# Eight pairs by seven quarter products in place of six, in the first MLP product of an encoder layer

## The chip, the cores and the metric

The kernel runs on one core of one Trainium2 chip. The metric is the device time of one execution in microseconds (us), given as the median of several runs. The engines are called as in the profile: PE (TensorE, matrix products), PEld (its weight loads), DVE (VectorE), ACT (ScalarE), POOL (GpSimd) and SP (SyncE, which here only issues DMAs).

## What is computed

One layer of a streaming encoder: four token mixers, a cross-attention, and a gated MLP, for 512 tokens of width 1024 in float32. The change lies in the MLP, whose inner width is 2816:

```python
hf = _rms_norm(x, norm_ffn_pre[l])
u = _dwconv_causal(hf @ w_up[l], ffn_dw[l]) + ffn_dw_b[l]
u_g, u_v = jnp.split(u, 2, axis=-1)
yff = (jax.nn.silu(u_g) * u_v) @ w_down[l]
x = x + _rms_norm(yff, norm_ffn_post[l])
```

The first MLP product is `hf @ w_up`. Column block j of 128 columns exists twice, once as gate and once as value; the two are called pair j, and there are 22 pairs (0 to 21).

## The kernel before

**Numbers.** Each float32 operand is split into a high part (an ACT cast to a shorter format, `wh`) and the rest (a DVE subtraction, `wl`). A product is three matmuls per block of 128 rows: high by high, high by low, low by high (`mm3`, line 240).

**A plain pair** takes two weight tiles of 128x1024 (gate, value), and per tile 8 row blocks x 3 matmuls of 512 columns: 48 such matmuls. DVE then adds two shifted taps of the convolution (line 597), ACT gives the first tap with its bias and the silu (lines 1612, 1618), DVE multiplies gate by value (line 1619).

**A pair by seven quarter products** treats gate and value, two halves of the inner width and two halves of the tokens as 2x2 blocks, and replaces eight block products by seven (names A11, A12, S1, S2, S3, S4, A22), at the price of sums. Each product has 4 row blocks x 3 matmuls of 256 columns: 84 such matmuls for the pair. The sums of token parts are made once (`token_terms`). The sums of weights are four DVE additions per pair (lines 1691 to 1694, tiles `su`, `wv`, `s4`), the sums of results are three ACT copies and three DVE additions to `u` (line 1684), with one more copy.

**A turn.** `SEVEN_AT` lists the pairs j that are done in this way, and each such pair shares a turn with the plain pair j+1 (`seven_jobs`, line 1665 on). A turn has five weight tiles, split in this order. I call them by a letter:

- F: A11 and A12 (from `wg`)
- G: the gate tile of pair j+1 (from `wr`)
- S: S1 and S2 (from `su`)
- T: S3 and A22 (from `wv`)
- V: the value tile of pair j+1 (from `wr`)

S4 has tiles of its own (`s4h`, `s4l`). F of turn 8 is written F8, and so on. A turn does 84 matmuls of 256 columns and 48 of 512.

**Slots.** Split weights have four slots (`weights_tile`): the n-th weight tile of the program takes slot n mod 4, so its ACT cast waits until PE has done the last matmul on the tile four before it. With turns back to back, V of a turn follows F of that turn in its slot, F of the next turn follows G, the next G follows S, the next S follows T, and the next T follows V:

```python
        return w_tiles.pop((kind, i), None) or gp.tile([P, WB], F32R, tag=f"{kind}{i % 4}", name=kind)
```

Raw weights from HBM have two buffers (`wr`), loaded by SP; `wg`, `wv`, `su` and the tiles of the next paragraph (`wp`) share a ring of seven buffers.

**Steps.** During the first product, the kernel also prepares the weights of the second one (`Sums`, line 530 on): for each of 11 row pairs q, POOL loads two tiles `wp` from `w_down`, DVE does four operations on them (lines 545 to 548), POOL stores them to `sums`. Each call of `step()` does the next load, the next four operations or the next store: two loads, then 11 times add, store and (9 times) load, 33 in all. A turn calls `step()` four times, a plain pair twice from pair 3 on.

**Order.** The program is written in turn order, and a scheduler then places the instructions of each engine by a model of its own, once, when the kernel is built. On the chip every engine takes its instructions in that fixed order.

Of the kernel before, what the change touches and what calls it, by code (L numbers as in the profile page):

```python
# [36 lines left out]
WB = 2 * 520  # L37
LINE = 256
HALF_SHIFT = 16
SEVEN_AT = (4, 7, 10, 13, 16, 19)  # L40
BIG = -float(2.0 ** 100)
LAMBDA_INIT = 0.8 - 0.6 * math.exp(-0.3 * 0)

# [41 lines left out]
def hybrid_layer(ctx: ExitStack, tc: tile.TileContext, a: dict, out: bass.AP):  # L85
# [12 lines left out]
    def bank(tag=None):  # L98
        if tag is None:
            turn_of.n += 1  # L100
            tag = "av" if turn_of.shared and turn_of.n % 2 else "mm"
        return psum.tile([P, 512], F32, tag=tag, name=f"ps_{tag}", bufs=2)
# [50 lines left out]
    def split(ps, hi, lo, scale=None):  # L153

        if scale is None:
            A.copy(hi, ps)  # L156
            V.tensor_tensor(lo, ps, hi.bitcast(F32), ALU.subtract)  # L157
        else:
            A.activation(hi, ps, AF.Copy if isinstance(scale, float) else AF.Identity, scale=scale)
            V.scalar_tensor_tensor(lo, ps, scale, hi.bitcast(F32), ALU.mult, ALU.subtract)  # L160
# [19 lines left out]
    def split_weights(raw, shape, low=V, order=same, shift=0):  # L180

        n = int(math.prod(shape[1:]))
        hi, lo = weights_tile("wh"), weights_tile("wl")
        names = "k c" if len(shape) == 3 else "c"
        form = f"p ({names}) -> p {names}"

        def view(t):
            return t.rearrange(form, k=shape[1]) if len(shape) == 3 else t

        hi, lo = hi[:, shift:shift + n], lo[:, shift:shift + n]  # L190
        order(A.copy(hi, raw[:, :n]))  # L191
        low.tensor_tensor(lo, raw[:, :n], hi.bitcast(F32), ALU.subtract)  # L192
        return view(hi), view(lo)
# [38 lines left out]
    def matmul(ps, lhs, rhs, start, stop, more=False):  # L232
        PE.matmul(ps, lhs, rhs, start=start, stop=stop, skip_group_check=more)  # L233
        bg.clock += max(int(math.prod(rhs.shape[1:])), 256) * 0.00042
# [1331 lines left out]
    def ring(dtype=F32, name="dw"):  # L1566
        return ns.fp.tile([P, D], dtype, tag="dw", name=name, bufs=7)
# [37 lines left out]
    def up_jobs():  # L1605
        st, held = {}, []
        seven = SEVEN_AT
        raws = {}

        def first_and_taps(c, j, i, src):  # L1610
            ch = i * NF + j
            st["first"] = A.activation(c[:, i], src, AF.Identity, bias=pc("fb", ch), scale=pc("fdw2", ch)).ins
            st["taps"] = taps(c[:, i], src, lambda k: pc("fdw01", k * 44 + ch), 3).ins
# [8 lines left out]
        def done(j, i, ps):  # L1622
            if i == 0:
                st[j] = ns.fp.tile([P, 2, S], F32, tag="c", name="c", bufs=2)
            first_and_taps(st[j], j, i, ps)
            if i == 1:
                gated(st[j], j)
# [14 lines left out]
        def step(n=1):  # L1642
            for _ in range(n):
                f, q = next(steps, (None, None))
                if f == ns.sums.add:
                    with tc.issue_after(st["taps"]):
                        f(q)
                elif f is not None:
                    f(q)

        def half_sums(ps, w, ks):
            hi, lo = w
            for k in ks:
                mm3(ps, hi[:, k], lo[:, k], ns.hf[0][:, k], ns.hf[1][:, k], k == 0, k == NK - 1)
# [4 lines left out]
        def load_pair(j):  # L1659
            if j in seven:  # L1660
                raws[j] = [ring(name="wg"), ring(name="wv")]
                for i, raw in enumerate(raws[j]):
                    SP.dma_start(raw.rearrange("p (k c) -> p k c", k=NK), plain(j, i)[0])

        def seven_jobs(j):
            n, tok = j + 1, [slice(i * S // 2, (i + 1) * S // 2) for i in range(2)]
            w, x, kept = {}, {}, {}
            old = lambda k, t: [h[:, 4 * k:4 * k + 4, tok[t]] for h in ns.hf]

            def weights(name, raw):  # L1670
                hi, lo = split_weights(raw, [P, NK, P], V, same, HALF_SHIFT)
                for i, m in enumerate(name):
                    w[m] = hi[:, 4 * i:4 * i + 4], lo[:, 4 * i:4 * i + 4]
                return ()

            def product(ps, name, b, first=True):
                hi, lo = w[name]
                for k in range(4):
                    for i, (w_p, x_p) in enumerate(((hi, b[0]), (hi, b[1]), (lo, b[0]))):
                        matmul(ps[:, :S // 2], w_p[:, k], x_p[:, k], first and i == k == 0, i == 2 and k == 3,  # L1680
                               not first)

            def add(dst, ps):
                V.tensor_tensor(dst, dst, ps[:, :S // 2], ALU.add)

            def first_weights():
                g, v = raws[j]
                su, s4 = kept["su"], kept["s4"] = ring(name="su"), ns.fp.tile([P, S], F32, tag="s4", name="s4")
                weights(("A11", "A12"), g)
                with tc.issue_after(st["taps"]):  # L1690
                    V.tensor_tensor(su[:, :S], v[:, :S], v[:, S:], ALU.add)
                V.tensor_tensor(su[:, S:], su[:, :S], g[:, :S], ALU.subtract)
                V.tensor_tensor(v[:, :S], g[:, :S], v[:, :S], ALU.subtract)
                V.tensor_tensor(s4, g[:, S:], su[:, S:], ALU.subtract)
                return [()]

            def second_weights():
                load_pair(seven[seven.index(j) + 1] if j < seven[-1] else None)
                weights(("S1", "S2"), kept["su"])
                return [()]  # L1700

            def third_weights():
                weights(("S3", "A22"), raws.pop(j)[1])
                hi, lo = (ns.fp.tile([P, S + 64], F32R, tag=f"s4{m}", name=f"s4{m}") for m in "hl")
                hi, lo = (m[:, HALF_SHIFT:HALF_SHIFT + S] for m in (hi, lo))
                split(kept["s4"], hi, lo)
                w["S4"] = tuple(m.rearrange("p (k c) -> p k c", k=4) for m in (hi, lo))
                return [()]

            def first(_):  # L1710
                u = kept["u"] = ns.fp.tile([P, 2, 2, S // 2], F32, tag="u", name="u", bufs=2)
                x.update(x=bank("sc"), v=bank("sc"), w=bank("tr"))
                product(x["x"], "A11", old(0, 0))
                A.copy(u[:, 0, 0], x["x"][:, :S // 2])
                product(x["w"], "A12", old(1, 0))
                add(u[:, 0, 0], x["w"])

            def gate_first(hi, lo):
                x["n"] = bank(), (hi, lo)
                half_sums(*x["n"], range(4))  # L1720
                step()

            def second(_):
                product(x["x"], "S2", ns.terms[1], False)
                A.copy(kept["u"][:, 1, 0], x["x"][:, :S // 2])
                step()

            def third(_):
                u = kept["u"]
                product(x["v"], "S3", ns.terms[2])  # L1730
                half_sums(*x["n"], range(4, NK))
                done(n, 0, x["n"][0])
                product(x["x"], "S1", ns.terms[0], False)
                A.copy(u[:, 1, 1], x["x"][:, :S // 2])
                add(u[:, 1, 1], x["v"])
                step()

            def value(hi, lo):
                u, ps = kept["u"], bank()
                half_sums(ps, (hi, lo), range(4))  # L1740
                product(x["x"], "S4", old(1, 1), False)
                A.copy(u[:, 0, 1], x["x"][:, :S // 2])
                half_sums(ps, (hi, lo), range(4, NK))
                done(n, 1, ps)
                step()
                product(x["v"], "A22", ns.terms[3], False)
                add(u[:, 1, 0], x["v"])
                c = ns.fp.tile([P, 2, S], F32, tag="c", name="c", bufs=2)
                for i in range(2):
                    first_and_taps(c, j, i, u[:, i].rearrange("p a b -> p (a b)"))  # L1750
                gated(c, j)

            yield first_weights, None, first
            yield *plain(n, 0), gate_first, V, same, 0
            yield second_weights, None, second
            yield third_weights, None, third
            yield *plain(n, 1), value, V, same, 0
# [30 lines left out]
        j = 0  # L1788
# [250 lines left out]
```

## Time and profile before

| | us |
|---|---|
| median of 3 runs | 1046.9 (1046.65 to 1046.99) |
| the profiled execution's own time | 1047.96 |
| its span, first to last instruction | 1046.2 |
| PE busy | 1036.5 (99%) |
| DVE busy | 836.9 (80%) |
| ACT busy | 530.6 (51%) |
| turn 4's first product starts, from the span's start | 743.9 |

The profiled execution lies 1.06 us above the median, and 1.8 us of its time lie outside of the span. All rows quoted in the prediction are of this one execution. A row of the timeline gives start, duration, engine, line, operation, destination and sources, and in brackets how long the engine stood idle before it and what ended that.

### The profile page before, as it was taken

How to read it: one execution, taken by the hardware profiler on the slowest of the kernel's cores; microseconds unless marked ns; L12 is line 12 of the kernel's file. 1: busy time of each engine (PE TensorE's matmuls, PEld its weight loads, DVE VectorE, ACT ScalarE, POOL GpSimd, SP SyncE). 2: the span in 40 equal slices, each digit the busy share in tenths (PEclk: the TensorE clock that was granted, in tenths of full speed). 3: DMA queues.
4: the chain of work that ended last, by engine and by line, in shares of the span. 5: the costliest groups of instructions: out<-in, count | busy, mean ns of one | idle time of the engine just before them, and what ended most of it. 6: DMA issues, size and time to landing. Idle time of an engine off the chain costs nothing.

```text
span 1046.2 us, 15153 instructions
## 1 busy us (share of the span) xinstructions
PE 1036.5 (99%) x5511; PEld 891.6 (85%) x5511; DVE 836.9 (80%) x1386; ACT 530.6 (51%) x894; POOL 181.6 (17%) x309
## 2 busy tenths in 40 slices
PE   9999999999999999999999999999999999999997
PEld 8888888888888988888888899999888888888886
DVE  6899998667667567767577888788898888889996
ACT  5322222277565356655443665676445443566772
POOL 4000000300230334342112033020011111000031
PEclk9999999999999999999999999999999999999999
DMA  7953433652343263322457743246577767757652
GB/s 254 301 177 104 104 101 125 188 131 81 106 134 95 76 177 102 101 83 79 121 153 229 267 136 122 81 138 206 174 229 242 237 218 233 242 176 220 199 175 81
DMA packets 166528, 167.31 MB, mean 160 GB/s; under 512 B 6655, under 2 KB 136300, under 8 KB 166197
## 3 DMA queue, kind: packets, MB, share of 16 engines
q1 hardware_dynamic: 154147, 124.10, 39.8%
q0 software_dynamic: 12160, 42.10, 12.0%
q8 instruction: 43, 0.70, 0.3%
q14 instruction: 32, 0.26, 0.1%
q10 hardware_dynamic: 146, 0.14, 0.0%
HBM read 141.13 MB, written 25.18 MB: 159 GB/s over the span
## 4 chain that ended last, share of the span: by engine, by line
PE 98%; DMA 1%; DVE 0%; issue 0%; ACT 0%; POOLq 0%; DVEq 0%; POOL 0%; SPq 0%; ACTq 0%
PE ps_mm L233 48%; PE ps_av L233 28%; PE ps_sc L233 13%; PE ps_tr L233 5%; PE ps_tr L237 2%; DMA wide<-in_w_out 1%; PE ps_mm L445 1%; PE ps_mm L387 0%; PE ps_sc L392 0%; PE ps_av L445 0%; ACT hth L156 0%; DVE o L1923 0%; PE ps_tr L429 0%; DVE wide L546 0%; POOLq L2035 0%
## 5 line engine op out<-in xcount | busy, mean ns | idle before, releaser
L191 ACT CAST wh<-wr 128x1024 fp32r<-128x1024 f32 (+1 forms) x130 | 136.3, 1050 | 235.8 <-PE ps_mm L233 129.2
L192 DVE TENSOR_TENSOR wl<-wr,wh 128x1024 fp32r<-128x1024 f32 (+1 forms) x130 | 161.1, 1241 | 65.5 <-ACT wh L191 65.3
L233 PE MATMUL ps_mm<-hth,wh 128*128 128x512 f32 (+1 forms) x544 | 202.6, 380 | 0.2 <-ACT hth L156 0.2
L233 PE MATMUL ps_mm<-htl,wh 128*128 128x512 f32 (+1 forms) x544 | 202.4, 379 | 0.0
L233 PE MATMUL ps_mm<-hth,wl 128*128 128x512 f32 (+1 forms) x544 | 202.1, 379 | 0.0
L233 PEld LDWEIGHTS ps_mm<-hth,wl 128*128 128x128 f32 x544 | 100.5, 188 | 18.2
L233 PEld LDWEIGHTS ps_mm<-hth,wh 128*128 128x128 f32 x544 | 100.6, 188 | 17.8 <-ACT hth L156 0.8
L233 PEld LDWEIGHTS ps_mm<-htl,wh 128*128 128x128 f32 x544 | 100.6, 188 | 17.0
L233 PE MATMUL ps_av<-hth,wh 128*128 128x512 f32 (+1 forms) x304 | 113.2, 373 | 0.0
L233 PE MATMUL ps_av<-htl,wh 128*128 128x512 f32 (+1 forms) x304 | 113.2, 372 | 0.0
L233 PE MATMUL ps_av<-hth,wl 128*128 128x512 f32 (+1 forms) x304 | 113.1, 372 | 0.0
L668 DVE SCALAR_TENSOR_TENSOR y<-y,par,y 128x482 f32<-128x482 f32 (+29 forms) x120 | 83.3, 735 | 0.1
L233 PEld LDWEIGHTS ps_av<-hth,wl 128*128 128x128 f32 x304 | 57.1, 188 | 10.0
L233 PEld LDWEIGHTS ps_av<-hth,wh 128*128 128x128 f32 x304 | 57.2, 188 | 9.7
L233 PEld LDWEIGHTS ps_av<-htl,wh 128*128 128x128 f32 x304 | 57.1, 188 | 9.8
L1808 ACT CAST wh<-dw 128x1024 fp32r<-128x1024 f32 x32 | 33.2, 1050 | 18.3 <-PE ps_tr L233 9.0
L269 POOL TENSOR_TENSOR st_m<-pm,nhalf 128x1 f32<-128x1 f32 x12 | 13.5, 1128 | 159.5 <-ACT junk L1878 90.4
L1809 DVE TENSOR_TENSOR wl<-dw,wh 128x1024 fp32r<-128x1024 f32 x32 | 39.0, 1222 | 2.8 <-ACT wh L1808 2.3
L1061 POOL TENSOR_SCALAR fbias<-ck,cq 128x128 f32<-128x128 f32 (+3 forms) x32 | 28.2, 890 | 63.0 <-DVE st L1068 56.6
L156 ACT CAST pth<-ps_tr 128x512 fp32r<-128x512 f32 (+3 forms) x56 | 23.5, 448 | 24.9 <-PE ps_tr L237 24.7
L233 PE MATMUL ps_sc<-t,wh 128*128 128x256 f32 x168 | 32.8, 278 | 0.0
L157 DVE TENSOR_TENSOR ptl<-ps_tr,pth 128x512 fp32r<-128x512 f32 (+3 forms) x56 | 27.5, 512 | 6.0 <-ACT pth L156 5.7
(553 smaller groups left out, 2453.2 us busy)
## 6 DMA issues: line engine op xcount, KB each, us to landing
wr<-in_w_in SPq DMA_DIRECT2D x38, 512.0 KB
wr<-in_w_gate SPq DMA_DIRECT2D x32, 512.0 KB
wr<-in_w_up SPq DMA_DIRECT2D x32, 512.0 KB
wp<-in_w_down POOLq DMA_DIRECT2D x22, 512.0 KB, 4.6
sums<-wp POOLq DMA_DIRECT2D x22, 512.0 KB, 3.7
dw<-sums SPq DMA_DIRECT2D x44, 256.0 KB
wr<-in_w_branch SPq DMA_DIRECT2D x16, 512.0 KB
wide<-in_w_out SPq DMA_DIRECT2D x12, 512.0 KB
```

The lines of the kernel that those rows point to most:

```text
L156: A.copy(hi, ps)
L157: V.tensor_tensor(lo, ps, hi.bitcast(F32), ALU.subtract)
L191: order(A.copy(hi, raw[:, :n]))
L192: low.tensor_tensor(lo, raw[:, :n], hi.bitcast(F32), ALU.subtract)
L233: PE.matmul(ps, lhs, rhs, start=start, stop=stop, skip_group_check=more)
L237: PE.transpose(ps, x, ident[:n, :n])
L269: G.tensor_tensor(m, parts[0], eps[:, :n], ALU.add)
L445: keep(PE.matmul(banks[c][:, :S // 2], w[p == 1][:, k, c * P:(c + 1) * P], ht[p == 2][:, i * 4 + k, :S // 2], start=(i, p, k) == (0, 0, 0) ...
L668: ins = V.scalar_tensor_tensor(dst[:, s:], src[:, :S - s], pc("conv_dw", k * 4 + j), dst[:, s:], ALU.mult, ALU.add)
L1061: G.tensor_scalar(bias[:, :w], ck[j][:, :w], -1.0, cq[:, qt, head:head + 1], ALU.mult, ALU.add)
L1808: A.copy(hi, x)
L1809: parts["low"] = V.tensor_tensor(lo, x, hi.bitcast(F32), ALU.subtract).ins
```

## The change

Turns are at pairs 4, 6, 8, 10, 12, 14, 16 and 19 in place of 4, 7, 10, 13, 16 and 19. So the plain pairs 6, 9, 12 and 15 between turns go, pair 18 remains, and seven turns follow each other directly. In the turns at 4, 6 and 8, `step()` is called a fifth time, in `first`.

```diff
-SEVEN_AT = (4, 7, 10, 13, 16, 19)
+SEVEN_AT = (4, 6, 8, 10, 12, 14, 16, 19)
...
                 A.copy(u[:, 0, 0], x["x"][:, :S // 2])
+                if j < 10:
+                    step()
                 product(x["w"], "A12", old(1, 0))
```

The scheduler places the instructions anew. Two places matter below. Numbers in names tell tiles apart.

**First place: the end of turn 6.** On ACT before, this is how the cast of T7 (`wh_7611`) stood; that of G7 (`wh_7532`) stood ten rows ahead of it:

```order
L191 CAST wh_7573<-su_7453 128x1024 [waits PE_49]
L1618 ACTIVATE c_7521<-c_7521 128x512 [waits DVE_49,Activation_49]
L1612 ACTIVATE c_7561<-ps_mm_7536,par2_411 128x512 [waits DVE_49,PE_49]
L191 CAST wh_7611<-wv_7278 128x1024 [waits DMAHW6_49,PE_49]
L1612 ACTIVATE c_7561<-ps_av_7577,par2_411 128x512 [waits PE_49]
```

Now, on ACT, `wh_7753` is T8, which takes the slot of V of turn 6, `wh_7628` is G8, which takes the slot of S6, and `c_7656` belongs to pair 7:

```order
L191 CAST wh_7601<-wg_7459 128x1024 [waits DMAHW0_49,PE_49]
L1612 ACTIVATE c_7656<-ps_mm_7584,par2_411 128x512 [waits PE_49]
L1727 COPY u_7544<-ps_sc_7545 128x256 [waits PE_49]
L191 CAST wh_7753<-wv_7460 128x1024 [waits DVE_49,DMAHW2_49,PE_49,Activation_49]
L1618 ACTIVATE c_7656<-c_7656 128x512 [waits DVE_49,Activation_49]
L191 CAST wh_7628<-wr_7626 128x1024 [waits DMAHW1_49,PE_49]
```

T8's cast now stands two rows ahead of G8's. On PE before, after the last of the 12 matmuls of A12 (into `ps_tr`), the first matmul with a new gate tile has no wait of its own left:

```order
L233 MATMUL ps_tr_7622<-htl_6456,wh_7455 128x256
L233 MATMUL ps_tr_7622<-hth_6455,wl_7456 128x256
L233 MATMUL ps_mm_7655<-hth_6455,wh_7532 128x512
L233 MATMUL ps_mm_7655<-htl_6456,wh_7532 128x512
L233 MATMUL ps_mm_7655<-hth_6455,wl_7533 128x512
```

Now, on PE, the last matmul of V6 (`ps_av_7686`) is followed by the 12 of A12 of turn 8, and the last of these by the first with G8:

```order
L233 MATMUL ps_tr_7764<-htl_6456,wh_7601 128x256
L233 MATMUL ps_tr_7764<-hth_6455,wl_7602 128x256
L233 MATMUL ps_mm_7801<-hth_6455,wh_7628 128x512 [waits Activation_49]
L233 MATMUL ps_mm_7801<-htl_6456,wh_7628 128x512
L233 MATMUL ps_sc_7545<-hth_6455,s4h_7540 128x256 [waits Activation_49]
```

So the first G8 matmul now waits for ACT itself, and A12 of the next turn runs ahead of S4 of this one.

**Second place: the start of turn 10.** On ACT before, the cast of V of turn 10 (`wh_7943`, in the slot of F10) came right behind the copy of A11's result:

```order
L1618 ACTIVATE c_7853<-c_7853 128x512 [waits DVE_49,Activation_49]
L1714 COPY u_7911<-ps_sc_7912 128x256 [waits PE_49]
L191 CAST wh_7943<-wr_7941 128x1024 [waits DMAHW7_49,PE_49]
L1725 COPY u_7911<-ps_sc_7912 128x256 [waits PE_49]
L191 CAST wh_7964<-wr_7962 128x1024 [waits DMAHW0_49,PE_49]
```

Now, on ACT, `wh_7899` is S10 (in the slot of T8), `wh_8033` is F12 and `wh_8012` is V10:

```order
L191 CAST wh_7899<-su_7818 128x1024 [waits PE_49]
L1612 ACTIVATE c_8088<-ps_mm_8016,par2_411 128x512 [waits DVE_49]
L191 CAST wh_8033<-wg_7895 128x1024 [waits DMAHW1_49]
L1612 ACTIVATE c_7963<-u_7761,par2_411 128x512 [waits DVE_49]
L191 CAST wh_8012<-wr_8010 128x1024 [waits DMAHW7_49,PE_49]
L1714 COPY u_7980<-ps_sc_7981 128x256 [waits PE_49]
```

Four ACT operations that start with S10's cast now stand ahead of V10's. On PE, now, S3 of turn 10 (`ps_sc_7982`) is followed by two matmuls of A12 of turn 12 and then by V10; before, the 24 of V stood behind the last of their gate tile. The rows now:

```order
L233 MATMUL ps_sc_7982<-t0_7146,wl_7973 128x256
L233 MATMUL ps_tr_8196<-hth_6455,wh_8033 128x256 [waits Activation_49]
L233 MATMUL ps_tr_8196<-htl_6456,wh_8033 128x256
L233 MATMUL ps_av_8118<-hth_6455,wh_8012 128x512 [waits Activation_49]
L233 MATMUL ps_av_8118<-htl_6456,wh_8012 128x512
L233 MATMUL ps_sc_7981<-t6_7142,wh_7899 128x256 [waits Activation_49]
```

Both V10's first matmul and F12's first wait for ACT.

## The prediction

> **What bounds the kernel now.** I read the busy times first, then the chain of work that ended last, then the stretches of the first MLP product one by one.
>
> ```profile
> PE 1036.5 (99%) x5511; PEld 891.6 (85%) x5511; DVE 836.9 (80%) x1386; ACT 530.6 (51%) x894; POOL 181.6 (17%) x309
> ...
> PE 98%; DMA 1%; DVE 0%; issue 0%; ACT 0%; POOLq 0%; DVEq 0%; POOL 0%; SPq 0%; ACTq 0%
> ```
>
> PE is busy throughout and is the chain that ends last. The windows of two whole periods (a turn and the plain pair behind it; columns are length, then busy time of PE, PEld, DVE, ACT and POOL, granted clock, DMA share, GB/s) say the same of the place of the change: PE never rests there, DVE rests 31.63 - 27.03 = 4.60 us.
>
> ```profile
> 786.08:817.70 31.62, 31.62 (x181) 27.77 (x181) 27.03 (x38) 14.96 (x21) 4.26 (x8) 1.00 0.73 233
> 817.70:849.33 31.63, 31.63 (x182) 27.78 (x181) 27.03 (x38) 14.95 (x21) 3.19 (x6) 1.00 0.68 217
> ```
>
> So time can be won only by giving PE less to do, and is lost wherever PE comes to wait. The chain gives PE's pace (start, length, what):
>
> ```profile
> 801.88 5.44 PE ps_av L233 x24
> 807.32 1.41 PE ps_sc L233 x12
> 808.73 1.41 PE ps_tr L233 x12
> ...
> 833.51 5.44 PE ps_av L233 x24
> ```
>
> 24 matmuls of 512 columns take 5.44 us, 0.227 each. 12 of 256 take 1.41, 0.118 each. A period is 833.51 - 801.88 = 31.63.
>
> **What PE is spared.** A plain pair is 2 x 5.44 = 10.88. A period holds two plain pairs and one pair by seven, so the latter takes 31.63 - 21.76 = 9.87 (84 x 0.118 agrees: 9.9). Each pair changed over saves 1.01, two save **2.02 us**. This is PE's whole gain; the bytes from HBM and the 33 steps stay the same in number, so nothing else gets shorter on the path.
>
> **What DVE gets.** A turn alone lasts 31.63 - 10.88 = 20.75 on PE. DVE's own pace is read from starts, since one operation's record runs on into the next:
>
> ```profile
> 782.67 0.69 DVE L547 TENSOR_TENSOR wp<-wp 128x512 f32<-128x512 f32 x1
> 783.40 0.69 DVE L548 TENSOR_TENSOR wp<-wp 128x512 f32<-128x512 f32 x1
> ...
> 795.30 1.22 DVE L192 TENSOR_TENSOR wl<-wr,wh 128x1024 fp32r<-128x1024 f32 x1
> 796.44 0.69 DVE L1694 TENSOR_TENSOR s<-wg,su 128x512 f32<-128x512 f32 x1
> 797.04 0.74 DVE L597 SCALAR_TENSOR_TENSOR c<-ps_av,par,c 128x510 f32<-128x510 f32 x1
> 797.70 0.68 DVE L548 TENSOR_TENSOR wp<-wp 128x512 f32<-128x512 f32 x1
> 798.30 0.74 DVE L597 SCALAR_TENSOR_TENSOR c<-u,par,c 128x510 f32<-128x510 f32 x1
> 798.96 0.41 DVE L1684 TENSOR_TENSOR u<-u,ps_sc 128x256 f32<-128x256 f32 x1
> 799.29 0.74 DVE L597 SCALAR_TENSOR_TENSOR c<-ps_av,par,c 128x511 f32<-128x511 f32 x1
> ```
>
> From start to start a weight tile's low part takes 1.14, an operation of 512 columns 0.60, a tap 0.66, an addition to `u` 0.33. A turn has 5 low parts (5.7), 7 operations of 512 (four weight sums, the low part of S4, two gated products: 4.2), 8 taps (5.3) and 3 additions (1.0): 16.2 us. Four steps of the sums of `w_down` per turn are 4/3 of a row pair at 4 x 0.60 = 2.4, so 3.2; five steps are 4.0. DVE is then busy 19.4 us, in turns 4, 6 and 8 20.2 us, of PE's 20.75. Before, it was 27.03 of 31.63. So DVE keeps up on the whole, with 0.5 to 1.3 us of rest per turn. I cost its added work (about 5 us per changed pair) at nothing, because PE's matmuls cover it; without that cover it would cost what exceeds 20.75, which the second rival takes up. POOL's two more DMAs per row pair come at the same rate of steps; SP's five loads per turn of two pairs replace loads of the same bytes.
>
> **What the tighter turns add: waits for a slot.** Slots rule when a split can begin. The clearest case of before is a cast that waits for PE's last matmul on the slot, and the low part that waits for the cast:
>
> ```profile
> 786.56 1.05 ACT L191 CAST wh<-wr 128x1024 fp32r<-128x1024 f32 x1 [2.60 <-PE ps_mm L233]
> ...
> 787.64 1.23 DVE L192 TENSOR_TENSOR wl<-wr,wh 128x1024 fp32r<-128x1024 f32 x1 [3.56 <-ACT wh L191]
> ```
>
> These waits cost nothing before, since PE needed the tile only several us later. With the plain pair gone, a release and the need of the next tile come closer, and then the rows ahead of a cast on ACT count. ACT's pace, again from start to start:
>
> ```profile
> 796.85 0.82 ACT L1612 ACTIVATE c<-u,par 128x512 f32<-128x512 f32 x1
> 797.57 0.61 ACT L156 CAST s4h<-s 128x512 fp32r<-128x512 f32 x1
> ...
> 807.13 1.05 ACT L191 CAST wh<-wv 128x1024 fp32r<-128x1024 f32 x1 [3.19 <-PE ps_av L233]
> 808.08 0.77 ACT L1612 ACTIVATE c<-ps_av,par 128x512 f32<-128x512 f32 x1
> 808.75 0.62 ACT L1618 ACTIVATE c<-c 128x512 f32<-128x512 f32 x1
> 809.27 0.36 ACT L1714 COPY u<-ps_sc 128x256 f32<-128x256 f32 x1
> ```
>
> A cast passes on after 0.95 and is done after 1.05; the first tap from PSUM passes on after 0.67, from `u` after 0.72, a silu after 0.52.
>
> I went through the new order of ACT, DVE and PE turn by turn with these paces. Two places come out late.
>
> *End of turn 6* (first place of the change's section). T8's cast needs V6's slot, which PE frees with the last matmul of V6. Behind T8's cast on ACT stand a silu and G8's cast, though G8's slot has been free before that. From V6's end: 0.95 + 0.52 + 1.05 = 2.52 until G8 is cast. PE has only A12 of turn 8 to do in between, 12 x 0.118 = 1.41. PE waits **1.11 us**. DVE is held too, by T8's low part ahead of G8's, but G8's low part is ready about 0.5 before PE gets to it.
>
> *Start of turn 10* (second place). From the end of A22 of turn 8, ACT does S10's cast, a first tap from PSUM, F12's cast, a first tap from `u`, V10's cast: 0.95 + 0.67 + 0.95 + 0.72 + 1.05 = 4.34. PE has A11 and S3 of turn 10 and two matmuls, 1.41 + 1.41 + 0.24 = 3.06. PE waits **1.28 us**.
>
> At the other turns I find the cast in time, by 0.2 us at the least (S4 of turn 14, behind G16's cast) and mostly by 1 to 5. The ends for each of the two waits are 0 (PE's true position and ACT's differ from my count by over 1.2) and about 3 (ACT held further by a late DMA, below); I take the counted values, for which every term has a row.
>
> **Sum.** -2.02 + 1.11 + 1.28 = **+0.37 us**. From the profiled execution's 1047.96 this is 1048.3; that execution stands 1.06 above the median, so 1047.3 in terms of the median. The change would move the time by under 0.1%. About 0.2%, 2.1 us, is what a measurement of this kernel can tell from no change.
>
> **Rival one: no waits, the whole gain.** If the two casts come in time, 1046.9 - 2.0 = 1044.9. For it: before, PE waited for nothing in this stage, and a term of 1.2 us is only a few operations of ACT. Against it: the order of rows is fixed, and each term is a measured pace.
>
> **Rival two: DVE becomes the bound, slower.** The point is 20.75 us of DVE per turn. If operations followed each other not by 0.60 but by their recorded length and a gap (0.73 between lines 547 and 548 above, where one reads what the other wrote), the turn would hold 5 x 1.22 + 7 x 0.69 + 8 x 0.74 + 3 x 0.41 = 18.1 and 3.7 or 4.6 of sums: 21.8, early 22.7. PE would lose 1.0 in four turns and 1.9 in three, 9.7 in all, less 2.0: 1054.6. Against it: other rows of before follow at 0.60, and in the new order dependent operations mostly have others between them.
>
> [...]
>
> **Rival three: late loads, slower.** `wg`, `wv` and `wp` share seven buffers, and one round of the ring shrinks from 31.63 to about 23 us. A load of before, from its issue to the cast that waited for it, took 762.05 - 757.21 = 4.84, though in some stretches the DMA engines are full:
>
> ```profile
> 757.21 0.37 SPq L177 DMA_DIRECT2D wr<-in_w_up  x1
> ...
> 762.05 1.05 ACT L191 CAST wh<-wr 128x1024 fp32r<-128x1024 f32 x1 [2.39 <-DMA wr<-in_w_up]
> ...
> 771.00:775.00 4.00, 4.00 (x19) 3.34 (x18) 4.00 (x7) 1.30 (x3) 0.53 (x1) 1.00 1.02 351
> ```
>
> `wg` of turn 12 can be loaded only when the low part of T10 is done; by my count it then lands some 2 us before ACT wants it, in turns 14 and 16 some 3 to 4 before. If a landing took twice as long, 9.7, PE would lose 2.6 + 1.5 + 1.0, about 5 us: 1052. It decides from a landing time of 7 us on.
>
> **How the numbers follow.** Forecast, two waits about as counted: 0.55. Rival one: 0.20; with my 2.02 read from chain rows of two decimals, a third of it falls beyond 2.1 us. Rival two: 0.06. Rival three: 0.12. More waits of the forecast's kind than two, 1049 to 1051: 0.07. Faster by over 0.2% (below 1044.8): 0.07. Slower by over 0.2% (above 1049.0): 0.06 + 0.12 + 0.07 and a little of the forecast, 0.27. Within: 0.66. The range goes from 1044.7, just beyond rival one, to 1050.5, which leaves out rival two, about half of rival three and little else.
>
> **What would show it.** In the new profile, PE should wait for ACT `wh` twice, by 1.1 us some 5 us into turn 8's stretch (near 784, before the first `ps_mm` matmul behind twelve `ps_tr`) and by 1.3 us near 817 (first `ps_av` matmul of turn 10), and 84 + 48 matmuls should pass in 20.75 elsewhere. DVE should be busy 94 to 97% in the turns, with starts 0.60 apart. No wait of PE at all means rival one. DVE without rest and PE waiting for DVE `wl` in turn after turn means rival two. ACT or DVE waiting for DMA `wg` or `wp` there means rival three. My count is wrong altogether if PE's waits stand in other turns than 6 to 10.

## The result, and the profile after

The changed kernel takes **1050.42 us** in the median of 13 runs (1048.6 to 1053.16), the kernel before 1046.97 (1046.09 to 1047.8, 13 runs). The ratio is 1.0034 with a 95% interval of 1.0025 to 1.0042: slower by 0.34%. The profiled execution is one of 1050.42 us with a span of 1048.6. Busy times and chain of waits on its page:

```profile
PE 1036.1 (99%) x5583; PEld 894.4 (85%) x5583; DVE 846.0 (81%) x1404; ACT 535.1 (51%) x906; POOL 166.5 (16%) x309
...
PE 94%; DVE 2%; DMA 1%; issue 1%; ACT 1%; POOL 0%; POOLq 0%; DVEq 0%; ACTq 0%
```

PE's busy sum hardly fell, though it has less to do, and the chain that ended last is no longer PE's alone. To find the place I cut each trace at two matmuls that both have: A11's first of turn 4, and the first of the second product. Before:

```profile
743.74:933.73 189.99, 189.99 (x1081) 166.91 (x1080) 161.68 (x231) 91.12 (x128) 21.84 (x41) 1.00 0.71 228
```

After:

```profile
742.08:935.51 193.43, 190.34 (x1153) 170.20 (x1152) 171.27 (x249) 95.79 (x140) 21.86 (x41) 0.99 0.70 225
```

This stretch, in which the change lies, went from 189.99 to 193.43, **3.44 us longer** where 2.02 shorter was due if PE never waited. The mean granted clock in it fell from 1.00 to 0.99. The second product with what follows grew by 0.68, from 1046.18 - 933.73 = 112.45 to 1048.64 - 935.51 = 113.13. (What lies ahead took 743.74 and 742.08; the change isn't in it, and it is between 741.9 and 743.4 in the kernels below. So the two parts of these single executions, 4.12 together, need not give the 3.45 between the medians.) In the middle of the stretch a whole turn runs as the prediction wanted:

```profile
850.08:870.84 20.76, 20.76 (x134) 18.79 (x133) 18.84 (x28) 10.26 (x16) 2.66 (x5) 1.00 0.55 187
```

So the loss isn't spread over the turns, and PE's waits name its place:

```profile
PE ps_tr L233 <- ACT wh L191: 1.9, 1, 1.9
...
PE ps_av L233 <- ACT wh L191: 1.1, 1, 1.1
PE ps_mm L233 <- DVE n L1811: 0.4, 1, 0.4
```

The third is in the second product. The first two are the start of turn 10. The rows of ACT and PE there:

```profile
811.59 1.05 ACT L191 CAST wh<-su 128x1024 fp32r<-128x1024 f32 x1 [0.92 <-PE ps_sc L233]
...
815.34 1.04 ACT L191 CAST wh<-wg 128x1024 fp32r<-128x1024 f32 x1 [2.02 <-DMA wg<-in_w_up]
816.29 0.81 ACT L1612 ACTIVATE c<-u,par 128x512 f32<-128x512 f32 x1
816.44 0.39 PE L233 MATMUL ps_tr<-hth,wh 128*128 128x256 f32 x1 [1.94 <-ACT wh L191]
...
817.01 1.03 ACT L191 CAST wh<-wr 128x1024 fp32r<-128x1024 f32 x1
...
818.09 0.50 PE L233 MATMUL ps_av<-hth,wh 128*128 128x512 f32 x1 [1.15 <-ACT wh L191]
```

ACT takes S10's cast, a tap, F12's cast, a tap and V10's cast in the order that front and prediction show. But F12's cast stood 2.02 us for its raw weights, and V10's cast, which had nothing of its own to wait for, stood behind it. The chain of waits says why the load was late:

```profile
804.97 1.14 DVE wl L192
...
806.12 9.19 DMA wg<-in_w_up
```

The buffer of the ring came free with T10's low part (the DVE row), as the third rival had it, and the load then took **9.19 us** to land, not the 4.84 of the row that I had priced it by. POOL's queue shows which transfers it shared that time with:

```profile
802.49 0.54 POOL L552 DMA_DIRECT2D sums<-wp  x1 [8.82 <-DVE wp L547]
803.34 0.53 POOL L541 DMA_DIRECT2D wp<-in_w_down  x1 [0.32 <-ACT u L1736]
804.92 0.54 POOL L552 DMA_DIRECT2D sums<-wp  x1 [1.05 <-DVE wp L548]
805.78 0.53 POOL L541 DMA_DIRECT2D wp<-in_w_down  x1 [0.32 <-DMA sums<-wp]
```

With a `wr` of SP's at 804.06 and the load itself these are six transfers of 512 KB within 3.6 us. Last, windows of two microseconds at and behind the two waits (the last three columns are granted clock, DMA share and GB/s):

```profile
816.00:818.00 2.00, 0.51 (x2) 0.30 (x2) 1.58 (x2) 2.00 (x4) 0.00 (x0) 1.00 1.06 397
...
820.00:822.00 2.00, 2.00 (x11) 2.00 (x11) 2.00 (x4) 0.54 (x2) 0.53 (x1) 0.50 0.78 260
822.00:824.00 2.00, 2.00 (x19) 2.00 (x18) 1.50 (x3) 0.36 (x1) 0.00 (x0) 0.98 0.85 286
```

The DMA engines are full (1.06) while PE is idle, and then another thing happens that I had not priced at all: the granted clock falls to 0.50, and PE does 11 matmuls in 2 us where it does 19 in the next window. PE's rows show the pace, 0.21 from start to start and then 0.12:

```profile
821.43 0.41 PE L233 MATMUL ps_tr<-hth,wh 128*128 128x256 f32 x1
821.65 0.41 PE L233 MATMUL ps_tr<-htl,wh 128*128 128x256 f32 x1
...
822.07 0.28 PE L233 MATMUL ps_tr<-hth,wh 128*128 128x256 f32 x1
822.19 0.28 PE L233 MATMUL ps_tr<-htl,wh 128*128 128x256 f32 x1
```

### The profile page after: what moved, and what is told of

It reads as the page before. It is cut to its first block, busy times and chain, and to the rows that moved or that the text cites. A ratio compares the mean times of both kernels' runs of the same rounds, so it can differ in the third digit from the quotient of the medians.

```text
span 1048.6 us, 15347 instructions
## 1 busy us (share of the span) xinstructions
PE 1036.1 (99%) x5583; PEld 894.4 (85%) x5583; DVE 846.0 (81%) x1404; ACT 535.1 (51%) x906; POOL 166.5 (16%) x309
## 4 chain that ended last, share of the span: by engine, by line
PE 94%; DVE 2%; DMA 1%; issue 1%; ACT 1%; POOL 0%; POOLq 0%; DVEq 0%; ACTq 0%
PE ps_mm L233 46%; PE ps_av L233 27%; PE ps_sc L233 13%; PE ps_tr L233 4%; PE ps_tr L237 3%; DMA wg<-in_w_up 1%; PE ps_mm L445 1%; PE ps_av L445 1%; DMA dw<-in_w_down 0%; PE ps_mm L387 0%; DVE wl L1811 0%; DVE n L1811 0%; DVE htl L1811 0%; PE ps_sc L392 0%; DVE wl L192 0%
## 5 line engine op out<-in xcount | busy, mean ns | idle before, releaser
L192 DVE TENSOR_TENSOR wl<-wr,wh 128x1024 fp32r<-128x1024 f32 (+1 forms) x126 | 156.2, 1242 | 52.2 <-ACT wh L191 51.9
L233 PE MATMUL ps_mm<-hth,wh 128*128 128x512 f32 (+1 forms) x528 | 196.4, 379 | 0.2 <-ACT hth L156 0.2
L233 PE MATMUL ps_mm<-hth,wl 128*128 128x512 f32 (+1 forms) x528 | 196.0, 379 | 0.0
L233 PE MATMUL ps_mm<-htl,wh 128*128 128x512 f32 (+1 forms) x528 | 195.9, 378 | 0.0
L233 PE MATMUL ps_av<-hth,wh 128*128 128x512 f32 (+1 forms) x288 | 107.1, 372 | 1.1 <-ACT wh L191 1.1
L233 PE MATMUL ps_av<-htl,wh 128*128 128x512 f32 (+1 forms) x288 | 107.0, 372 | 0.0
L233 PE MATMUL ps_av<-hth,wl 128*128 128x512 f32 (+1 forms) x288 | 106.8, 371 | 0.0
L233 PE MATMUL ps_sc<-t,wh 128*128 128x256 f32 x224 | 44.8, 284 | 0.0
L233 PEld LDWEIGHTS ps_sc<-t,wh 128*128 128x128 f32 x224 | 37.8, 193 | 2.0
L233 PE MATMUL ps_sc<-t,wl 128*128 128x256 f32 x128 | 36.0, 284 | 0.0
```

## The experiments

Two questions stood at the start. Does the late load come from the extra step, which brings loads and stores closer together? And is it the late load that costs, or the order in which F12's cast stands ahead of V10's? The times are medians, of 13 runs for the first two rows and 11 for the others, but 10 for two stores less, 6 for the old turns with the extra step and 5 for the extra step behind half of G. Each ratio is to runs of the kernel before that were made together with them, with medians between 1046.96 and 1047.14. "Stage" is the stretch from A11 of turn 4 to the second product in the profiled execution, "end" the one behind it, as in the windows above.

| kernel | stage | end | median | ratio to before, 95% |
|---|---|---|---|---|
| before | 189.99 | 112.45 | 1046.97 | |
| changed | 193.43 | 113.13 | 1050.42 | 1.0034, 1.0025 to 1.0042 |
| eight turns, no extra step | 187.90 | 113.34 | 1046.40 | 0.9992, 0.9983 to 1.0001 |
| old turns, extra step | 192.85 | 112.45 | 1050.30 | 1.0028, 1.0016 to 1.0040 |
| changed, V's cast ahead of F's on ACT | 189.34 | 114.06 | 1048.20 | 1.0014, 1.0005 to 1.0023 |
| seven turns with extra step | 190.57 | 112.47 | 1048.24 | 1.0008, 0.9999 to 1.0017 |
| extra step behind S2 | 188.92 | 112.44 | 1046.39 | 0.9991, 0.9982 to 1.0000 |
| extra step behind half of G | 193.06 | 112.73 | 1050.47 | 1.0038, 1.0025 to 1.0052 |
| extra step behind S1 | 188.97 | 112.45 | 1045.70 | 0.9986, 0.9977 to 0.9994 |
| extra step in turn 4 alone | 188.63 | 112.45 | 1046.87 | 1.0000, 0.9991 to 1.0009 |
| changed, two stores less | 190.10 | 114.09 | 1048.77 | 1.0011, 1.0002 to 1.0020 |
| changed, one store less | 189.65 | 112.49 | 1046.65 | 0.9995, 0.9986 to 1.0004 |
| old turns, extra step behind S1 | 190.21 | 112.45 | 1046.97 | 1.0002, 0.9993 to 1.0011 |

### The two halves of the change apart

Eight turns without the extra step:

```diff
-                if j < 10:
-                    step()
```

> The eight turns without the extra step. Theory one (the late load of F12's raw weights): POOL's loads and stores of the sums in turns 4 to 8 are fewer, so the crowd of DMAs around F12's load thins out; PE's wait for F12's cast falls from 1.9 us to under 1, no drop of the granted clock follows, and the time is about 1045 to 1046.5. Rival theory (the tighter turns alone make the load late, whatever the steps do): the wait of about 2 us for F12's cast and the lower clock stay, and the time is about 1050. Rival theory (order of ACT alone): here V10's cast stands ahead of F12's on ACT, so the second wait of 1.1 us goes and the time falls by about that, to 1049.

The time is 1046.40. PE waits nowhere in the stage, which takes 187.90: 2.09 less than before, for the 2.02 of the prediction. But the load of F12 is as late as ever. SP's and ACT's rows of this kernel:

```profile
806.19 0.57 SPq L1663 DMA_DIRECT2D wg<-in_w_up  x1
...
813.24 1.03 ACT L191 CAST wh<-wr 128x1024 fp32r<-128x1024 f32 x1
...
815.30 1.05 ACT L191 CAST wh<-wg 128x1024 fp32r<-128x1024 f32 x1 [0.75 <-DMA wg<-in_w_up]
```

815.30 - 806.19 = 9.1 us from issue to cast, much as in the changed kernel. Here V10's cast (`wh<-wr`) stands ahead of F12's on ACT, and on PE matmuls of V10 and S10 come ahead of F12's. So theory one, in the form in which it was put, falls, though the time came out as it said: the load is late without the extra step too. What is left of the theory needs the order as well.

The old turns with the extra step:

```diff
 SEVEN_AT = (4, 7, 10, 13, 16, 19)
...
+                if j < 10:
+                    step()
```

> The old six turns with the extra step. PE has the same matmuls as in the kernel before; each of the two early turns with j under 10 has one more step. Theory one: raw weights still come in time, as each turn is followed by a plain pair, so 1047.0, within 0.5 us of the kernel before. If the extra step costs by itself (DVE's or the DMA queues' time), it shows here as 1048 or more.

This was a miss: 1050.30, as slow as the changed kernel, though PE does the matmuls of the kernel before. The chain of waits of this kernel, and PE's wait at its end:

```profile
821.40 6.27 DMA sums<-wp
...
827.69 0.06 DVE su L1691
...
829.52 0.34 DVE u L1684
```

```profile
829.90 0.39 PE L233 MATMUL ps_sc<-t,wh 128*128 128x256 f32 x1 [1.03 <-DVE u L1684]
```

It is another wait at another place. (PE also waits 0.77 us at 814.37, for a copy to `u` on ACT, line 1714; what held that copy up I didn't follow.) The first of the weight sums (`su`, line 1691) takes a buffer of the ring of seven that a store of `sums` still reads; the store lands after 6.27 us; DVE waits 4.00 us for that, and the addition to `u`, for which PE waits, stands behind it on DVE. Taken alone the two halves seem to add up to the result (-0.6 and +3.3), yet the trace of the changed kernel has no wait of DVE for `sums` in the stage. That the sum nearly fits is a coincidence.

### The order on ACT

The changed kernel, with the cast of F of the next turn placed behind V's:

```diff
-                weights(("A11", "A12"), g)
+                if "cast" in st:
+                    with tc.issue_after(st["cast"]):
+                        weights(("A11", "A12"), g)
...
-            yield *plain(n, 1), value, V, same, 0
+            yield *plain(n, 1), value, V, note, 0
```

(`note` records V's cast in `st["cast"]`; where there is none yet, F is cast as before.)

> The changed kernel, but on ACT the cast of F of the next turn stands behind the cast of V of this turn; loads and steps are the same. Theory one (late load of F12): V10's cast no longer waits for the load, so PE can do V10's 24 matmuls (5.4 us) while the load lands; PE's idle time at the start of turn 10 falls from about 3 us to about 1 or less, the granted clock stays at 1.00, and the time is 1046 to 1047.5, though the load itself lands as late as before, 8 to 9 us after its issue. Rival theory (DVE's or the crowd's load as such is what costs): the time stays at 1049.5 or more. If only the order of ACT counted, the load's landing would not be seen as a wait of ACT at all.

1048.20, slower than I expected, but the stage is 189.34 in place of 193.43, although the load took up to 8.7 us (issued at 806.64, cast at 815.38). The longer of the two waits that remain there (the other is 0.2, for F12), and ACT's rows:

```profile
815.53 0.50 PE L233 MATMUL ps_av<-hth,wh 128*128 128x512 f32 x1 [0.51 <-ACT wh L191]
```

```profile
812.11 1.05 ACT L191 CAST wh<-su 128x1024 fp32r<-128x1024 f32 x1 [0.93 <-PE ps_sc L233]
...
814.44 1.03 ACT L191 CAST wh<-wr 128x1024 fp32r<-128x1024 f32 x1
```

This is the forecast's second wait with one operation less on ACT: S10's cast, two taps and V10's cast still take longer than PE's A11 and S3. The clock stayed at 1.00. The rest of the loss is at the end: 114.06 for 112.45, where PE waits for `n` in the second product. The waits there are 0.52 and 0.50; I haven't tested why they come.

### Seven turns

```diff
-SEVEN_AT = (4, 6, 8, 10, 12, 14, 16, 19)
+SEVEN_AT = (4, 6, 9, 11, 14, 16, 19)
```

> Seven turns at 4, 6, 9, 11, 14, 16, 19: plain pairs 8, 13 and 18 stand between, never more than two turns follow each other; extra step in turns 4, 6 and 9. PE is spared 1.01 us once. Theory one: the ring of seven turns more slowly where plain pairs stand, the load is in time, 1046.0. If any two turns in a row bring the late load, a wait of 2 to 3 us at one of the three pairs of turns, 1048 or more.

1048.24, a miss by 2 us. ACT waits for no load of `wg`, but PE waits once, 0.7 us, for an addition to `u` (`PE ps_sc` for `DVE u L1684`), since the first weight sum ahead of it on DVE stood for 5.65 us until a store landed:

```profile
836.90 0.69 DVE L1691 TENSOR_TENSOR su<-wv 128x512 f32<-128x512 f32 x1 [5.65 <-DMA sums<-wp]
```

It is what the old turns with the extra step showed.

### The same steps at other places

If order, not load, makes the loss, the extra step must be free to do when it stands elsewhere in the turn. By the end of each turn DVE, POOL and the DMA engines have then the same work behind them, though single transfers go out at other times.

Behind S2, behind the first half of G and behind S1 (each without the lines in `first`):

```diff
             def second(_):
...
                 A.copy(kept["u"][:, 1, 0], x["x"][:, :S // 2])
                 step()
+                if j < 10:
+                    step()
```

> The changed kernel with the extra step of turns 4, 6 and 8 called behind S2 (in second) instead of behind A11 (in first): the same steps are done by the end of each turn, so DVE and the DMAs carry the same load. The scheduler then places V10 ahead of F12 on ACT, and on PE all of V10's 24 matmuls ahead of F12's. Theory one as it now stands (a late load of F12, which costs only because F12 stands ahead of V10 in both orders): the load lands as late as before, PE does not wait for it, no loss in the stage, 1046 to 1046.8. Rival (the extra step's load on DVE and DMA costs by itself): the first product loses 2 us or more, 1049 to 1050.5.

```diff
             def gate_first(hi, lo):
...
                 half_sums(*x["n"], range(4))
                 step()
+                if j < 10:
+                    step()
```

> The same again with the extra step behind the first half of G (in gate_first). Here the scheduler leaves F12 ahead of V10 on ACT and PE, as in the changed kernel. Order theory: the same loss as in the changed kernel, some 5 us at the start of turn 10, about 1050. Rival (the place of the extra step in its turn counts, not the order at turn 10): the loss moves or goes.

```diff
             def third(_):
...
                 add(u[:, 1, 1], x["v"])
                 step()
+                if j < 10:
+                    step()
```

> The changed kernel with the extra steps of turns 4, 6 and 8 called behind S1 (in third). As many steps by the end of each turn as in the changed kernel; the scheduler places V10 ahead of F12 on both engines, as with the steps behind S2. Order theory: no loss at the start of turn 10, 1046 to 1046.8. Rival (the load of the extra steps): 1049 to 1050.5.

1046.39, 1050.47 and 1045.70: each as the order says. With the step behind G, F12's cast stands ahead of V10's on ACT, row for row as in the changed kernel's second place of the front part. With the step behind S2 or S1, V10's cast stands ahead of F12's, and PE has all 24 matmuls of V10 ahead of F12's. PE's waits in the stage with the step behind G, and its clock behind them:

```profile
PE ps_tr L233 <- ACT wh L191: 1.6, 1, 1.6
PE ps_av L233 <- ACT wh L191: 1.2, 1, 1.2
```

```profile
820.00:822.00 2.00, 2.00 (x11) 2.00 (x11) 2.00 (x3) 0.09 (x1) 1.05 (x2) 0.50 0.41 49
```

With the step behind S1 PE waits in the stage only once, 0.23 us for a copy to `u` (line 1725) in turn 12. The load of F12 is issued even later there, and PE doesn't wait for it:

```profile
808.32 0.37 SPq L1663 DMA_DIRECT2D wg<-in_w_up  x1
...
812.28 1.03 ACT L191 CAST wh<-wr 128x1024 fp32r<-128x1024 f32 x1
...
814.86 1.04 ACT L191 CAST wh<-wg 128x1024 fp32r<-128x1024 f32 x1
```

So the place of the step changes the load too: from issue to cast it took at most 814.86 - 808.32 = 6.5 us here, and 815.35 - 809.12 = 6.2 behind S2. Counted from the span's start, F12 was cast hardly sooner than the 815.34 of the changed kernel, with V10's cast ahead of it.

The kernel with the step behind S1 is **faster than the changed one, and by its interval than the one before**, 0.9986 (0.9977 to 0.9994); but these 1.3 us are less than the 2.1 that the prediction names as what can be told from no change. Its stage is 1.02 shorter than before, not 2.09: the wait of 0.23 us at turn 12 accounts for some of the difference, the rest I can't place.

The extra step in turn 4 alone (`if j < 6`), where the order is again V10 ahead of F12:

> The changed kernel with the extra step in turn 4 alone. The scheduler places V10 ahead of F12 on ACT and on PE, as without any extra step. Order theory: no wait of PE at the start of turn 10, stage about 188 to 189 us, 1046 to 1046.8. If a step more or less counted by its own load, the time would lie a third of the way from 1046.4 (no extra step) to 1050.4 (three), at 1047.7.

PE doesn't wait at turn 10, and the stage is 188.63, a third of a microsecond from the two above; it waits 0.25 once, at 857. The median, 1046.87, is just beyond what was expected, with a spread of 1045.05 to 1049.09 for which I have no cause.

The old turns with the step behind S1 in place of behind A11:

> The kernel before, with its old turns, and the extra steps behind S1 in turns 4 and 7; the same steps by the end of each turn as in the run with the old turns and the step behind A11, which took 1050.3. If it was the place that the step takes in the engines' orders and in the ring of seven that cost 3 us there (DVE's weight sum waited for a store to land), it is gone or another here, 1046.5 to 1048. If the steps' load cost it, 1050 again.

1046.97, the time of before, and PE waits nowhere in the stage (190.21). The two steps more cost nothing by themselves; the 3.3 us behind A11 came from that place.

### Is the late load needed?

The changed kernel without two stores ahead of F12's load, and then without one. Both leave out work that the layer needs: where sums of row pair 4 aren't stored, the second product reads those of row pair 3.

```diff
             for i, x in enumerate(self.held.pop(q)):
+                if q == 4 and self is ns.sums:
+                    continue
                 self.queue.dma_start(self.dram[q * P:(q + 1) * P, i * D:(i + 1) * D], x)
...
+            q = 3 if q == 4 and self is getattr(ns, "sums", None) else q
```

> The changed kernel without the two stores of the sums of row pair 4, which are issued 2 to 4 us ahead of F12's load; the second product takes the sums of row pair 3 in their place. Two of the six transfers of 512 KB in flight are gone. The scheduler then puts all 12 matmuls of F12 ahead even of S3, so PE wants F12 about 1.4 us earlier than in the changed kernel. Crowd theory (six transfers share the DMA engines' 350 GB/s): the load lands some 6 us after its issue in place of 9.2, PE waits for F12 under 1.5 us, and the time is 1045.5 to 1048. Rival (the load is late because its buffer comes free late, and lands in 9 us whatever else is in flight): PE waits some 3.4 us for F12, the clock drops, 1050 or more.

1048.77. F12's cast waited for PE alone, not for the load, which was there within 812.93 - 805.95 = 7.0 us:

```profile
812.93 1.05 ACT L191 CAST wh<-wg 128x1024 fp32r<-128x1024 f32 x1 [4.74 <-PE ps_sc L233]
```

PE waited 0.7 us for F12's low part and 0.8 at a later tile, and the end took 1.64 more, so the time is above what I expected, while the rival's 3.4 us and the fall of the clock are absent. As the order changed too, I took one store away, which leaves it as it was:

```diff
-                self.queue.dma_start(self.dram[q * P:(q + 1) * P, i * D:(i + 1) * D], x)
+                if not (q == 4 and i == 1 and self is ns.sums):
+                    self.queue.dma_start(self.dram[q * P:(q + 1) * P, i * D:(i + 1) * D], x)
...
+            q = 3 if q == 4 and self is getattr(ns, "sums", None) else q
```

> The changed kernel without the second of the two stores of the sums of row pair 4, issued 1.2 us ahead of F12's load; the second product takes the sums of row pair 3 in place of those of 4. ACT and PE have the same order as in the changed kernel at the start of turn 10, F12 ahead of V10. One of six transfers in flight is gone. If the transfers share the DMA engines, the load lands after some 7.7 us in place of 9.2, PE's wait for F12 falls from 1.9 us to about 0.5, the wait for V10 behind it stays at 1.1, no drop of the clock follows, and the stage loses about 2 us in place of 5.4: 1047 to 1047.8. If the order on ACT and PE alone made the loss, it stays: 1050 or more.

1046.65, a little below what I expected and 3.8 us less than the changed kernel, for one store of 512 KB that PE never needs in this stage. SP's and ACT's rows (lines are two further than in the changed kernel):

```profile
805.36 0.37 SPq L1665 DMA_DIRECT2D wg<-in_w_up  x1
...
813.01 1.04 ACT L191 CAST wh<-wg 128x1024 fp32r<-128x1024 f32 x1
```

```profile
PE ps_av L233 <- ACT wh L191: 1.2, 1, 1.2
```

The load was there in at most 813.01 - 805.36 = 7.65 us, F12's cast doesn't wait, and what is left is the forecast's second wait in its pure form, 1.15 us. The load was also issued 0.6 us earlier, against PE's position, since another buffer of the ring came free for it; of the 1.94 us by which PE's wait for F12 fell, so much isn't the shorter landing. Nor is the store the only difference: T12's load now goes out right behind F12's, at 805.92, where it is at 812.81 in the changed kernel. So one transfer less stood ahead of the load, not one less in all.

### What the clock follows

The kernel before, with copies of V's high part onto itself on ACT in turns 7, 10, 13 and 16, so that PE waits in a stage that otherwise has no wait (`HOLD` is 4, 7, 9, 11 copies, then 9, 10, 11, 13). Each ran once:

```diff
                 u, ps = kept["u"], bank()
+                for _ in range(HOLD.get(j, 0)):
+                    A.copy(hi, hi)
                 half_sums(ps, (hi, lo), range(4))
```

> The kernel before with 4, 7, 9 and 11 copies in place of V's high part on ACT in turns 7, 10, 13 and 16, so that PE comes to wait for V: idle times of different length in a stage that otherwise has none. If the granted clock drops by the length of PE's idle time, it falls to about a half for some 3 to 4 us behind idle times from some 2 to 3 us on, and stays at 1.00 behind shorter ones; if the clock's fall in the changed kernel had another cause, such as the DMAs' load, no drop is seen behind any of them.

> The kernel before with 9, 10, 11 and 13 copies in place of V's high part on ACT in turns 7, 10, 13 and 16. With 9 copies and V behind all else of its turn PE waited 1.6 us and the clock stayed at 1.00. Here PE should wait some 1.6, 2.5 and 3.5 us in turns 7, 10 and 13. If the clock follows the length of one idle time, it halves for some 3 to 4 us behind the longer of these, and the length at which it starts is read off; if it does not fall even behind 3.5 us, the clock's fall in the changed kernel isn't the idle time's.

The scheduler put other matmuls in most of the gaps, so that the waits are fewer and shorter than I wanted. Besides single ones of 0.3 to 0.5 us there is one of 1.60 in the first kernel, and in the second one of 1.69 with another of 0.52 four matmuls behind it. The first:

```profile
862.80 0.50 PE L233 MATMUL ps_av<-hth,wh 128*128 128x512 f32 x1 [1.60 <-ACT wh L1741]
```

```profile
863.00:865.00 2.00, 2.00 (x10) 1.60 (x10) 2.00 (x4) 2.00 (x4) 1.02 (x2) 1.00 0.81 332
```

The second:

```profile
895.45 0.39 PE L233 MATMUL ps_sc<-hth,wh 128*128 128x256 f32 x1 [1.69 <-ACT wh L191]
...
896.71 0.39 PE L233 MATMUL ps_sc<-hth,wl 128*128 128x256 f32 x1 [0.52 <-DVE wl L192]
```

```profile
897.00:899.00 2.00, 2.00 (x13) 2.00 (x13) 1.90 (x3) 1.93 (x4) 0.00 (x0) 0.58 1.00 137
899.00:901.00 2.00, 2.00 (x11) 1.95 (x11) 1.67 (x4) 1.08 (x3) 0.00 (x0) 0.57 0.87 324
```

The clock stays at 1.00 behind 1.60 us of idleness and is 0.58 and 0.57 in two windows of 2 us behind 1.69 and 0.52, in a program without the changed kernel's extra steps. Full DMA engines alone didn't bring the fall: the prediction's window from 771 to 775 has 1.02 at a clock of 1.00. So the fall came with PE's idleness, in these few cases. Single waits of over 1.7 us did not come about, so it isn't shown what the clock does behind one.

## Why the prediction was wrong

It said no change, 1047.3, with a range up to 1050.5; the kernel came out slower, at the edge of the range. That 1050.42 still lies inside is luck: one wait of the sum isn't there, while a longer one, the clock's fall and the second product's growth, none of them in the sum, are. Step by step:

**What PE is spared: right.** 2.02 was said; the eight turns without extra step show 2.09 in the stage.

**What DVE gets: right in the main.** A turn takes 20.76 us (20.75 was said), with DVE busy 18.84 of it, 91% and less than the 94 to 97% that I put. Rival two didn't occur, and starts are still 0.60 apart in the changed kernel (852.74 to 853.34):

```profile
852.74 0.68 DVE L157 TENSOR_TENSOR s4l<-s,s4h 128x512 fp32r<-128x512 f32 x1
853.34 0.74 DVE L597 SCALAR_TENSOR_TENSOR c<-ps_av,par,c 128x511 f32<-128x511 f32 x1
```

**Wait one, end of turn 6, 1.11 us: wrong, it isn't there.** I let T8's cast start with the last matmul of V6. But V6's last matmul reads only the low part; the high part's slot, which the cast takes, was free a whole S1 earlier. The rows of ACT and PE in the changed kernel:

```profile
779.55 1.05 ACT L191 CAST wh<-wv 128x1024 fp32r<-128x1024 f32 x1 [4.46 <-PE ps_av L233]
...
780.72 0.39 PE L233 MATMUL ps_av<-hth,wl 128*128 128x512 f32 x1
...
781.03 1.03 ACT L191 CAST wh<-wr 128x1024 fp32r<-128x1024 f32 x1
...
782.31 0.40 PE L233 MATMUL ps_mm<-hth,wh 128*128 128x512 f32 x1
```

T8's cast began 1.17 us ahead of V6's last matmul (780.72), and G8's was done at 782.06, before PE came to it at 782.31. What is left there is 0.2 us: G8's low part, which I had ready 0.5 ahead, ended only at 784.18, and the matmul that takes it and the next one started late by about 0.1 each.

**Wait two, start of turn 10, 1.28 us: right in mechanism and size**, 1.15 in the changed kernel and in the one with a store less. What I left out: from start to start the matmuls are held up by 0.28 more than these 1.15 (see the last section).

**That all other tiles come in time: the step that failed.** "By my count it then lands some 2 us before ACT wants it" was F12's load, with a landing of 4.84 from a row with few other transfers about. I had quoted a window with the DMA engines full (1.02), and still took the lighter row for the sum. Measured are 9.19, with six transfers within 3.6 us, and ACT stood 2.02 us for the load in place of having it 2 us early. Rival three had the buffer, the place and the deciding point (7 us) right, and got 0.12: ACT was free for F12's cast at 815.34 - 2.02 = 813.32, 7.2 us behind the load's issue. Its price was not right: it let PE lose time for three loads, and PE waited for one.

**The clock: not in the prediction at all.** Behind 3.09 us of idleness PE ran at the slow pace for 3.4 us, with a granted clock of 0.50; 16 matmuls of 256 columns at 0.213 in place of 0.118 are 1.5 us. That is over a quarter of the 5.5 us between this stage and the 187.90 of the eight turns without the extra step.

Put together from measured terms, the stage should move by -2.09, + 1.94 and 1.15 for the waits, + 0.56 for twice 0.28, + 1.5 for the clock: +3.06 of the 3.44 seen; 0.2 of the rest is the two matmuls near 784, and 0.2 I can't place. The second product adds 0.7, mostly through a wait of 0.40 for `n` that I had no term for; the end comes out between 112.4 and 114.1 in the kernels above, and I haven't tested why.

What the runs show as cause is a product, not a sum: a load that lands 9 us after its issue, *and* an order in which ACT and PE want it ahead of a tile that is already there. Against the 187.90 of the stage with neither wait, either alone costs little: late load with the other order, nothing (no extra step) or 1.4 us (V's cast ahead of F's); the order with a load that landed in at most 7.65 us, 1.7 us (one store less); both, over 5 (changed, and step behind half of G). In the kernels with eight turns the extra step cost over 1.5 us in this stage only where F12's cast came ahead of V10's. That the scheduler's model takes the load for earlier than it is, is an argument from the order, and not shown.

## What to carry to other kernels

Price a transfer by what will be in flight with it after the change, not by a row of before: closing up a schedule can close up its transfers too, and here a landing nearly doubled (4.84 to 9.19). Look at what stands behind each waiting instruction in an engine's fixed order, since here the late tile cost most where a ready one was queued behind it. And when a small edit passes through a scheduler, try the same edit at neighbouring places before judging it: here the same step cost 4 us behind A11 (1050.42 against the 1046.40 without it) and nothing behind S1 (1045.70).

## What the runs showed of the hardware

- In these traces the granted clock fell behind waits of PE that came close together. Behind 1.94 + 1.15 us (changed), 1.6 + 1.2 (step behind G) and 1.69 + 0.52 (copies on ACT) the lowest window of 2 us has 0.50, 0.50 and 0.57; behind 1.60 or 1.15 alone, and 0.51 + 0.22, the clock stayed at 1.00. So the longest single wait doesn't tell these cases apart: 1.6 with 1.2 behind it came ahead of a fall, and 1.60 by itself, in the one execution there is, didn't. The least idleness with a fall behind it was 2.21 us, in two parts. In the changed kernel PE is busy again from 818.09, the slow pace starts at 818.7, and from 822.07 on PE has its old pace. The fall doesn't show in every execution: 11 of 13 executions of the changed kernel have a mean clock of 0.995 or 0.996, two have 0.998 and 0.999, and these are its fastest, 1048.6 and 1049.06; whether PE waited as long in these two isn't known. All five executions with the step behind G have 0.994 to 0.996.
- A load of 512 KB took 4.84 us where I read it before; 9.1 to 9.2 in the changed kernel and the one without the extra step, in both as the last of six transfers issued within 3.6 to 3.8 us; at most 7.65 with one store less ahead of it, and at most 7.0 with two less.
- The two waits at turn 10 in the changed kernel cost PE some 0.28 us more than their rows say. Around the wait of 1.15 matmuls start at 816.66, 818.09, 818.43 and 818.66, 2.00 us in place of 0.118 + 2 x 0.227 = 0.57, so that 1.43 are lost. Around the wait of 1.94 they start at 814.21, 816.44 and 816.66, 2.45 us in place of 2 x 0.118 = 0.24, so that 2.21 are lost. In both rows the wait begins only where the record of the matmul ahead ends, 0.28 us behind its start.
